# Long GpSimd operations in pieces of 256 elements, and two tiles of a top-k search decided on ScalarE

## The chip, the cores and the metric

The kernel runs on one core of a Trainium2 chip. The metric is the device time of one execution in microseconds. A core has a matrix engine (TensorE, PE in the profile), two elementwise engines (VectorE, DVE; GpSimd, POOL), an engine for activation functions (ScalarE, ACT) and a queue that issues most transfers (SP). Each engine works through its own instructions in order and waits on semaphores for the others.

## The reference, cut to what matters

A trunk of two layers over 1024 tokens of width 1024. Layer 0 projects the tokens and feeds two groups of heads: RWKV-7 (a recurrence over chunks of 64 tokens) and sparse attention, in which an index score selects at most 256 keys for each query. Layer 1 is gated linear attention. Each layer ends with an output projection and a layer norm.

The part that the change's second edit touches is the selection:

```python
score = jnp.einsum('bqh,bqhs->bqs', wib, jax.nn.relu(jnp.einsum('bqhd,bsd->bqhs', qib, ki)))
score = jnp.where(adm[None], score, -jnp.inf)      # only keys of the same or an earlier chunk of 64
vals, idx = lax.top_k(score, top_k)                # top_k = 256
...
s = jnp.where(valid[:, :, None, :], s, -1e30)
p = jax.nn.softmax(s, axis=-1)
```

The first edit touches elementwise work in all stages: the split of fp32 weights into a rounded part and a rest, decayed operands, masks, the shift at the end of a layer norm.

## The kernel before, in words

Weights and activations are split into two float32r parts, `hi` and `lo`, and a product takes three matmuls (L143 to L145, L165 to L167, L728 to L730). ScalarE rounds `hi` (L128) and GpSimd subtracts (L129), 128 x 512 at a time, in `wload`; in `wcols` (blocks of 8 x 128 columns) GpSimd does both, L153 and L154. Of both there are a few buffers, so a split is made ahead of the matmuls that read it.

Layer 0 runs in this order. Index scores and queries (until L441; the rests of the queries' split are L344 and L424 on GpSimd). Then the RWKV projections for four pairs of heads j: `proj` fills two PSUM banks (`dn`), ScalarE copies them out (L471, or L461 for a gate), DVE adds the shifted part (L472) or forms the gate (L462). `norms`, `decays` and `operands` make the chunks' decayed operands; L553 and L556 there are GpSimd's. Pairs 0 to 2 stand in the program before the top-k search, pair 3 and three gates behind it (L693 to L711).

The search (`search`, L631 to L654) finds, for each query of the tiles 2 to 7 of 128 queries, the largest threshold that at least 256 keys reach. It works on ordered integer keys, 16 bits at a time, so it is called twice (L656, L664), with 16 bits each. For each bit and each of the tiles 2 to 5, DVE counts the keys that reach the trial threshold (L641); two small operations then keep or drop the bit for all four tiles (L645, L646). For the tiles 6 and 7 ScalarE counts, by a sum of signs (L650), and DVE decides with two one-element operations per tile (L652, L653), for which ScalarE's next count of that tile waits. Behind the search DVE makes the selection's mask `bias_s` (L684 to L691).

Then come attention and the RWKV chunks, interleaved by hand (`att`, `slot`): `substitute` masks on GpSimd (L950, L972) around a chain of small GpSimd operations (L964, L965); head norms (`normed_heads`, L1075) run on DVE with `rsqrt` (L107 to L119), a chain of small operations. Output projection, layer norm (`normed`, L732: the last addition, L744, is GpSimd's), layer 1 with its gates (`gate_piece`, L1354 on GpSimd), output projection and layer norm end the kernel.

The order of the instructions on each engine is not the program's: `tile.TileContext(nc, schedule_with_timeline_sim=True)` (L1471) lets a planner lay them out by priority (the program's order) and by its own prices, so projections and the search are interleaved on DVE and ScalarE.

The lines of the search that the change edits:

```python
A.activation(ajunk[:, :n], x, AF.Sign, bias=c[:, z:z + 1], accum_out=cnt[:, z:z + 1])        # L650
V.tensor_scalar(step[:, zz], cnt[:, zz], float(2 * TOPK - n), bit, op0=ALU.is_lt, op1=ALU.mult)   # L652
V.scalar_tensor_tensor(c[:, zz], step[:, zz], -dn, c[:, zz], op0=ALU.add, op1=ALU.add)       # L653
```

Of the kernel before, what the change touches and what calls it, by code (L numbers as in the profile page):

```python
# [8 lines left out]
F32 = mybir.dt.float32  # L9
# [4 lines left out]
AF = mybir.ActivationFunctionType  # L14
ALU = mybir.AluOpType
AX = mybir.AxisListType
# 2 pi in parts: the products of the first two with an integer below 2^16 are exact
# [46 lines left out]
def trunk(ctx: ExitStack, tc: tile.TileContext, x, positions, e_w_in, a_mu, a_w0, a_w2, a_a0, a_a2,  # L64
# [7 lines left out]

    def dump(name, ap):
        if dbg and name in dbg:
            nc.sync.dma_start(dbg[name], ap)
# [31 lines left out]
    def rsqrt(pool, xin, n, tag):  # L107
        """1 / sqrt(xin) for positive xin, [P, n]"""
        y = pool.tile([P, n], F32, name=tag + "y", tag=tag + "y", bufs=2)
        xh = pool.tile([P, n], F32, name=tag + "h", tag=tag + "h", bufs=2)  # L110
        u = pool.tile([P, n], F32, name=tag + "u", tag=tag + "u", bufs=2)
        V.tensor_scalar(u.bitcast(I32), xin.bitcast(I32), 1, None, op0=ALU.logical_shift_right)
        V.tensor_scalar(y.bitcast(I32), u.bitcast(I32), -1.0, float(0x5f3759df), op0=ALU.mult, op1=ALU.add)
        V.tensor_scalar(xh, xin, -0.5, None, op0=ALU.mult)
        for _ in range(3):
            V.tensor_mul(u, y, y)
            V.tensor_mul(u, u, xh)
            V.scalar_tensor_tensor(y, u, 1.5, y, op0=ALU.add, op1=ALU.mult)  # L118
        return y  # L119

    # ================= weights: streamed, split exactly into two float32r parts =================
    def wload(wr, w, c0, n, k, raws=3, bufs=9, scale=None, sub=G):
# [4 lines left out]
        if scale is None:  # L127
            A.copy(hi, raw)  # L128
            sub.tensor_sub(lo, raw, f32(hi))  # L129
        else:  # L130
            A.activation(hi, raw, AF.Copy, scale=scale(k))
            V.scalar_tensor_tensor(lo, raw, scale(k), f32(hi), op0=ALU.mult, op1=ALU.subtract)
# [5 lines left out]
    def mm_fm(pst, wb, cs, ah, al, half):  # L138
        """pst [cols, 512] = w[:, cols]^T act[half]"""
# [7 lines left out]
    def wcols(pool, w, c0):  # L147
        """128 columns of w"""
# [5 lines left out]
        G.tensor_sub(lo, raw, f32(hi))  # L154
# [14 lines left out]
    def transpose_split(src, ah, al, t, k0=0, nk=NK, banks=("tr", "tr")):  # L169
        """src [128 tokens, nk*128] into the feature-major split pair at token tile t"""  # L170
# [10 lines left out]
    # scratch in DRAM  # L181
# [11 lines left out]
    # ================= layer 0 =================  # L193
# [103 lines left out]
    def rope(X, nt, nh, half, t0, step):  # L297
        """X [P, nt, nh, head dim], rotated in place"""
# [40 lines left out]
    def index_queries(t):  # L339
# [4 lines left out]
        EN[QSE[0]].tensor_sub(qs[:, :, 1], qb, f32(qs[:, :, 0]))  # L344
# [68 lines left out]
    def queries(t0, wb):  # L413
# [6 lines left out]
        for t in range(4):  # L420
# [3 lines left out]
            EN[QSE[1]].tensor_sub(qs[:, :, 1], q3, f32(qs[:, :, 0]))  # L424
# [67 lines left out]
    def spill(dst, us, j, src):  # L492
        """the odd heads' halves change places"""
        nc.sync.dma_start(dst[0:CH, j, us, :], src[0:CH])
        for a, b in ((0, CH), (CH, 0)):
            nc.sync.dma_start(dst[CH:, j, us, a:a + CH], src[CH:, :, b:b + CH])
# [3 lines left out]
    def norms(j, k):  # L500
        """1 / the norms of the heads' keys, times the keys"""
# [12 lines left out]
    def decays(j, h, pool):  # L514
        """the rates and their running decays"""
# [16 lines left out]
    def operands(j, h, r, k, rn, dec, pool):  # L532
# [17 lines left out]
        if RK1:  # L550
            O(j, 7).tensor_mul(kk, r_, k_)
        # the chunks' decay, for the state's increments
        O(j, 6).tensor_mul(bk, bk, PC[:, j, h * 8:h * 8 + 8, None].to_broadcast([P, 8, P]))  # L553
        spill(d_bd, slice(h * 8, h * 8 + 8), j, bk)
        if not RK1:
            O(j, 7).tensor_mul(kk, r_, k_)  # L556
# [59 lines left out]
    nH = th.tile([P, NI], F32, name="nH")  # L616

# [13 lines left out]
    def search(data, c):  # L631
        """largest c with at least TOPK of data >= c; ACT's columns hold 1/2 - c"""
        V.memset(c[:, 0:ND], 0.0)
        V.memset(c[:, ND:], 0.5)
        for b in range(15, -1, -1):
# [7 lines left out]
            # c is tried with the bit set; it is taken back where too few are left  # L643
# [3 lines left out]
            for i in AT:  # L647
                x, z = data[:, rng(i)], i - 2
                n = P * (i + 1)
                A.activation(ajunk[:, :n], x, AF.Sign, bias=c[:, z:z + 1], accum_out=cnt[:, z:z + 1])  # L650
                zz = slice(z, z + 1)
                V.tensor_scalar(step[:, zz], cnt[:, zz], float(2 * TOPK - n), bit, op0=ALU.is_lt, op1=ALU.mult)  # L652
                V.scalar_tensor_tensor(c[:, zz], step[:, zz], -dn, c[:, zz], op0=ALU.add, op1=ALU.add)  # L653
        V.tensor_scalar(c[:, ND:], c[:, ND:], -1.0, 0.5, op0=ALU.mult, op1=ALU.add)  # L654
# [22 lines left out]
    for i in range(2, NT):  # L677
# [5 lines left out]
        # BIG where above the threshold, and for as many of its equals as are still needed, from the left; less BIG  # L683
# [48 lines left out]
    def normed(pool, z, gb):  # L732
        """z normalised in place"""
# [10 lines left out]
        G.tensor_add(z, z, gb[1])  # L744

# [16 lines left out]
    def att_logits(i, w):  # L762
        """exp of the selected logits less their maximum, and its sums; a generator of TensorE's bursts, in us"""
# [24 lines left out]
    def att_out(i, w):  # L788
# [9 lines left out]
        # the sums' inverses, along the features  # L798
# [31 lines left out]
    def attention():  # L830
        """every tile's output beside the next one's logits"""
# [25 lines left out]
    # source token by target token: after it, not before it  # L857
# [6 lines left out]
    # lane = row set * 64 + unit * 8 + parity * 4 + block; a lane holds the rows 2 m + set of its block  # L864
# [9 lines left out]
    # a row's own block  # L874
# [30 lines left out]
    def load_unit(u):  # L905
        """AT: a, r; in the other parity's rows k's products with a"""
# [15 lines left out]
    def products(u, cc):  # L922
        """the chunk's own products"""
# [21 lines left out]
    def substitute(u):  # L945
        """-(I + M)^-1: the 16 x 16 blocks on the diagonal by substitution, half of a block's rows per partition"""
# [3 lines left out]
        G.tensor_mul(mm, U_[u]["MAB"].rearrange("p v (b t) -> p v b t", t=HB), own_)  # L950
# [21 lines left out]
        G.tensor_mul(TT.rearrange("p v (b t) -> p v b t", t=HB), td[:, :, None, :].to_broadcast([P, 8, 4, HB]), own_)  # L972
# [5 lines left out]
    def offdiag(u, z):  # L978
        """the blocks above the diagonal: of 16 x 16 in those of 32 x 32, then of 32 x 32"""
# [43 lines left out]
    def chain(u, slot):  # L1023
        U = U_[u]
        Y = rt([P, 8, CH], "Y", 2)
        for cc in range(2):
# [16 lines left out]
            # rows: the odd heads' outputs, then the even heads'  # L1043
# [45 lines left out]
    def finish(t):  # L1089
        """the bonus and the gate"""  # L1090
# [3 lines left out]
        # the pair's heads lie behind one another, two pairs share the partitions  # L1094
# [19 lines left out]
    # the output projection, one tile of tokens by one half of the columns at a time; z before its layer norm  # L1114
# [149 lines left out]
    # ================= layer 1 =================  # L1264
# [10 lines left out]
    # gates of the decay: rank 16  # L1275
# [72 lines left out]
    def gate_piece(t, c, wb):  # L1348
# [5 lines left out]
        G.tensor_mul(vg[c][:, t], vg[c][:, t], o)  # L1354
# [120 lines left out]
```

## Time and profile before

| | |
|---|---|
| median of 3 runs | 1380.54 us (1375.79 to 1385.37) |
| profiled execution, its span from first to last instruction | 1379.4 us |
| busy: TensorE matmuls | 1243.3 us, 90% |
| busy: DVE | 847.8 us, 61% |
| busy: ScalarE | 564.0 us, 41% |
| busy: GpSimd | 421.1 us, 31% |
| mean granted TensorE clock | 0.949 of full speed |

For the profiled execution the span is what is recorded; what lies around it is not, and the runs' median is 1.1 us above it. The shares are means over stages with different limits: the stage between 187 and 450 us holds the search. A DVE row of a few hundred nanoseconds may overlap the next by some tens of nanoseconds, so what an instruction costs its queue is read from the distance of the starts.

### The profile page before, as it was taken

The page shows a single profiled execution, that of the slowest core. Times are in us where ns is not written, and L with a number is a line of the kernel's source. Part 1 is how long each engine was busy: PE and PEld are TensorE (multiplying, and loading weights), DVE is VectorE, ACT ScalarE, POOL GpSimd, SP SyncE. Part 2 cuts the span into 40 slices and gives each one's busy share as a digit, 9 for nine tenths or more (in the row PEclk, how much of TensorE's full clock was granted, in tenths as well). Part 3 has the DMA queues.
Part 4 walks back from the last instruction along what each step waited for, and adds up shares of the span by engine and source line. Part 5 has one row for each costly group of instructions (what it writes and reads, how often), then busy time and mean ns, then how long its engine had stood idle before and what let it go on. Part 6 is the DMA issues. An engine that isn't in the chain of part 4 may idle for free. (4 is left out here: it accounts for less than half of the span.)

```text
span 1379.4 us, 21874 instructions
## 1 busy us (share of the span) xinstructions
PE 1243.3 (90%) x8141; PEld 963.6 (70%) x8141; DVE 847.8 (61%) x2029; ACT 564.0 (41%) x1089; POOL 421.1 (31%) x532
## 2 busy tenths in 40 slices
PE   7997797887788988999999879899999999998996
PEld 6976585565566666677766658777578878887885
DVE  5345879999999456768767646683330114453665
ACT  5345757637532425555554432132551123333100
POOL 3313431341424351444444351153112221131122
PEclk9998798998899989999999989999899999999998
DMA  6102311431424378334433376561102220013131
GB/s 206 31 1 76 107 39 31 124 104 50 127 54 122 108 199 216 90 73 120 125 94 78 88 222 214 197 200 60 35 0 61 62 62 0 1 62 103 62 118 62
DMA packets 164634, 130.50 MB, mean 95 GB/s; under 512 B 61424, under 2 KB 138272, under 8 KB 164528
## 3 DMA queue, kind: packets, MB, share of 16 engines
q1 hardware_dynamic: 161728, 122.72, 30.9%
q10 hardware_dynamic: 2800, 6.39, 1.5%
q8 instruction: 64, 1.05, 0.3%
q14 instruction: 42, 0.34, 0.1%
HBM read 86.08 MB, written 42.99 MB: 94 GB/s over the span
## 5 line engine op out<-in xcount | busy, mean ns | idle before, releaser
L129 POOL TENSOR_TENSOR wlo<-wraw,whi 128x512 fp32r<-128x512 f32 (+1 forms) x80 | 100.7, 1275 | 191.2 <-ACT whi L128 126.5
L143 PE MATMUL dn<-xh,chi 128*128 128x512 f32 x336 | 137.6, 410 | 16.6 <-DVE sh L472 8.7
L145 PE MATMUL dn<-xh,clo 128*128 128x512 f32 x336 | 137.3, 409 | 0.0
L144 PE MATMUL dn<-xl,chi 128*128 128x512 f32 x336 | 136.8, 407 | 0.0
L128 ACT CAST whi<-wraw 128x512 fp32r<-128x512 f32 (+1 forms) x80 | 48.6, 613 | 130.9 <-PE dn L144 65.6
L143 PEld LDWEIGHTS dn<-xh,chi 128*128 128x128 f32 x336 | 65.8, 196 | 36.3 <-issue 11.3
L744 POOL TENSOR_TENSOR z<-z,ln 128x1024 f32<-128x1024 f32 x16 | 38.7, 2419 | 166.6 <-DVE z L743 83.2
L144 PEld LDWEIGHTS dn<-xl,chi 128*128 128x128 f32 x336 | 65.9, 196 | 20.9 <-issue 7.4
L145 PEld LDWEIGHTS dn<-xh,clo 128*128 128x128 f32 x336 | 65.8, 196 | 18.6 <-issue 5.0
L153 POOL CAST chi<-craw 128x1024 fp32r<-128x1024 f32 x21 | 25.8, 1231 | 133.3 <-PE dn L144 95.3
L380 DVE SCALAR_TENSOR_TENSOR sc<-rl,wi_s,sc 128x384 f32<-128x384 f32 (+5 forms) x42 | 50.6, 1205 | 24.4 <-ACT rl L375 22.4
L728 PE MATMUL s<-whi,yh 128*128 128x512 f32 x128 | 52.6, 412 | 14.0 <-DVE gny L118 7.1
L795 PE MATMUL po<-pT,v_tm 128*64 128x256 f32 x288 | 62.7, 400 | 0.0
L785 ACT ACTIVATE p<-p,am 128x128 f32<-128x128 f32 (+7 forms) x64 | 49.1, 769 | 18.6 <-DVE am L783 18.1
L154 POOL TENSOR_TENSOR clo<-craw,chi 128x1024 fp32r<-128x1024 f32 x21 | 54.5, 2595 | 0.9
L776 DVE CUSTOM_DVE_ANT_0 p<-s,bias_s 128x512 f32<-128x512 f32 (+1 forms) x80 | 45.4, 591 | 14.8 <-PE s L775 11.9
L729 PE MATMUL s<-wlo,yh 128*128 128x512 f32 x128 | 52.2, 408 | 0.3 <-POOL wlo L129 0.3
L641 DVE TENSOR_SCALAR_CACHE_REDUCE junk<-klo,Lc 128x384 bf16<-128x384 int16 (+1 forms) x64 | 51.8, 809 | 0.6
L641 DVE TENSOR_SCALAR_CACHE_REDUCE junk<-khi,Hc 128x384 bf16<-128x384 int16 (+1 forms) x64 | 51.8, 809 | 0.5
L1354 POOL TENSOR_TENSOR vg<-vg,sg 128x512 f32<-128x512 f32 x16 | 20.5, 1285 | 103.2 <-DVE vg L1399 66.8
L165 PE MATMUL gt<-whi,hh 128*128 128x512 f32 x128 | 51.9, 406 | 0.0
L730 PE MATMUL s<-whi,yl 128*128 128x512 f32 x128 | 51.5, 402 | 0.0
(470 smaller groups left out, 3429.1 us busy)
## 6 DMA issues: line engine op xcount, KB each, us to landing
wraw<-in_o_w_in_dram SPq DMA_DIRECT2D x48, 256.0 KB
craw<-in_e_w_in_dram SPq DMA_DIRECT2D x21, 512.0 KB
xt<-in_x_dram SPq DMA_DIRECT2D x8, 512.0 KB
d_q<-qiT SPq DMA_DIRECT2D x8, 512.0 KB
d_ar<-ar SPq DMA_DIRECT2D x8, 512.0 KB
d_gate<-sg SPq DMA_DIRECT2D x8, 512.0 KB
qT<-d_q SPq DMA_DIRECT2D x8, 512.0 KB
BK<-d_bk SPq DMA_DIRECT2D x8, 512.0 KB
```

The lines of the kernel that those rows point to most:

```text
L129: sub.tensor_sub(lo, raw, f32(hi))
L143: PE.matmul(pst, wh[:, cs], ah[:, k, sl], start=(k == 0), stop=False)
L144: PE.matmul(pst, wh[:, cs], al[:, k, sl], start=False, stop=False)
L145: PE.matmul(pst, wl[:, cs], ah[:, k, sl], start=False, stop=(k == NK - 1))
L154: G.tensor_sub(lo, raw, f32(hi))
L165: PE.matmul(pst, ah[:, k, sl], wh, start=(k == 0), stop=False)
L380: E.scalar_tensor_tensor(acc[:, a:b], r, w, acc[:, a:b], op0=ALU.mult, op1=ALU.add)
L641: V.tensor_scalar(junk[:, :n], x, c[:, z:z + 1], None, op0=ALU.is_ge, op1=ALU.add, accum_out=cnt[:, z:z + 1])
L728: PE.matmul(pt, yh[:, k, :], wh, start=(k == 0), stop=False)
L729: PE.matmul(pt, yh[:, k, :], wl, start=False, stop=False)
L730: PE.matmul(pt, yl[:, k, :], wh, start=False, stop=(k == NK - 1))
L795: inorder(PE.matmul(po[RS[s], c:c + PVN], v_tm[:, kt, :], pT[s][:, c:c + PVN], start=(kt == 0 and c == 0), stop=(kt == i), skip_group_chec ...
```

## The change

First edit: GpSimd's two-input operations of 512 or 1024 elements a partition are issued in pieces of at most 256 elements: `cut` slices the first free dimension. It applies to L129 (2 pieces, 80 calls), L154 (4, 21), L344 and L424 (2, 6 and 8), L553 (4, 8), L556 (2, 8), L744 (4, 16), L950 and L972 (2, 8 each) and L1354 (2, 16). GpSimd's one-input operations (L153, L544) and the small ones stay.

Second edit: for the tiles 6 and 7 of the search, L652 and L653 on DVE become two activations on ScalarE, on one element a partition. A constant column `odd` holds n - 2 * 256 + 1, so that the sign of count plus `odd` is never zero; half a bit times that sign is taken from the threshold.

```diff
+    PIECE = 256
+    def cut(f, out, *ins):
+        n = out.shape[1]
+        each = 1
+        for m in out.shape[2:]:
+            each *= m
+        w = max(1, PIECE // each)
+        for a in range(0, n, w):
+            f(out[:, a:min(n, a + w)], *(z[:, a:min(n, a + w)] for z in ins))
+    def gsub(out, a, b):
+        cut(G.tensor_sub, out, a, b)
...
-            sub.tensor_sub(lo, raw, f32(hi))
+            gsub(lo, raw, f32(hi))
...
-        G.tensor_sub(lo, raw, f32(hi))
+        gsub(lo, raw, f32(hi))
...
-        EN[QSE[0]].tensor_sub(qs[:, :, 1], qb, f32(qs[:, :, 0]))
+        gsub(qs[:, :, 1], qb, f32(qs[:, :, 0]))
...
-        O(j, 6).tensor_mul(bk, bk, PC[:, j, h * 8:h * 8 + 8, None].to_broadcast([P, 8, P]))
+        (gmul if j < OG[6] else V.tensor_mul)(bk, bk, PC[:, j, h * 8:h * 8 + 8, None].to_broadcast([P, 8, P]))
...
+    sg_ = th.tile([P, NI], F32, name="sg_")
+    odd = th.tile([P, NI], F32, name="odd")
+    for i in AT:
+        V.memset(odd[:, i - 2:i - 1], float(P * (i + 1) - 2 * TOPK + 1))
...
-                A.activation(ajunk[:, :n], x, AF.Sign, bias=c[:, z:z + 1], accum_out=cnt[:, z:z + 1])
                 zz = slice(z, z + 1)
-                V.tensor_scalar(step[:, zz], cnt[:, zz], float(2 * TOPK - n), bit, op0=ALU.is_lt, op1=ALU.mult)
-                V.scalar_tensor_tensor(c[:, zz], step[:, zz], -dn, c[:, zz], op0=ALU.add, op1=ALU.add)
-        V.tensor_scalar(c[:, ND:], c[:, ND:], -1.0, 0.5, op0=ALU.mult, op1=ALU.add)
+                A.activation(ajunk[:, :n], x, AF.Sign, bias=c[:, zz], accum_out=cnt[:, zz])
+                A.activation(sg_[:, zz], cnt[:, zz], AF.Sign, bias=odd[:, zz])
+                A.activation(c[:, zz], sg_[:, zz], AF.Identity, scale=-0.5 * bit, bias=c[:, zz])
+        V.tensor_scalar(c[:, ND:], c[:, ND:], -1.0, None, op0=ALU.mult)
...
-        G.tensor_add(z, z, gb[1])
+        gadd(z, z, gb[1])
```

## Rows read from the trace of the kernel before

**Rows 1.** The page's 40 slices of the span, busy tenths of TensorE and of DVE.

```profile
PE   7997797887788988999999879899999999998996
DVE  5345879999999456768767646683330114453665
```

**Rows 2.** Busy time by stretch. After the stretch: its length, then busy us and instructions of TensorE, its weight loads, DVE, ScalarE and GpSimd; the granted clock, the DMA share and GB/s.

```profile
187.00:292.00 105.00, 91.59 (x359) 68.47 (x358) 103.55 (x270) 66.62 (x103) 29.75 (x18) 0.92 0.27 77
292.00:391.00 99.00, 78.59 (x276) 56.30 (x275) 97.26 (x261) 58.69 (x92) 30.80 (x18) 0.86 0.33 93
391.00:450.00 59.00, 51.04 (x198) 36.45 (x197) 57.29 (x86) 15.13 (x20) 21.98 (x11) 0.97 0.31 90
450.00:500.00 50.00, 49.48 (x198) 36.01 (x199) 23.59 (x29) 16.68 (x22) 20.05 (x12) 1.00 0.47 121
...
850.00:960.00 110.00, 101.05 (x458) 81.07 (x458) 75.98 (x160) 25.45 (x46) 36.43 (x22) 0.98 0.47 154
```

**Rows 3.** TensorE's longest waits between 187 and 450 us: who waited for whom, us in total, times, longest.

```profile
PE ix L508 <- ACT sq L506: 11.2, 2, 7.2
PE dn L143 <- DVE sh L472: 8.7, 2, 5.3
```

**Rows 4.** Timeline of DVE within one bit of the first search: start us, duration us, engine, line, operation, tiles and shapes.

```profile
207.17 0.15 DVE L652 TENSOR_SCALAR step<-cnt 128x1 f32<-128x1 f32 x1
207.29 0.75 DVE L641 TENSOR_SCALAR_CACHE_REDUCE junk<-khi,Hc 128x512 bf16<-128x512 int16 x1
...
207.96 0.15 DVE L653 SCALAR_TENSOR_TENSOR Hc<-step,Hc 128x1 f32<-128x1 f32 x1
208.08 0.88 DVE L641 TENSOR_SCALAR_CACHE_REDUCE junk<-khi,Hc 128x640 bf16<-128x640 int16 x1
...
210.06 0.17 DVE L645 TENSOR_SCALAR step<-cnt 128x4 f32<-128x4 f32 x1
210.26 0.16 DVE L646 SCALAR_TENSOR_TENSOR Hc<-step,Hc 128x4 f32<-128x4 f32 x1
```

**Rows 5.** DVE's groups between 187 and 391 us, those of the decisions: busy us, mean ns of one, then idle before.

```profile
L645 DVE TENSOR_SCALAR step<-cnt 128x4 f32<-128x4 f32 x31 | 12.0, 387 | 0.1
L653 DVE SCALAR_TENSOR_TENSOR Lc<-step,Lc 128x1 f32<-128x1 f32 x32 | 10.2, 320 | 0.0
...
L653 DVE SCALAR_TENSOR_TENSOR Hc<-step,Hc 128x1 f32<-128x1 f32 x32 | 6.9, 216 | 0.0
...
L646 DVE SCALAR_TENSOR_TENSOR Hc<-step,Hc 128x4 f32<-128x4 f32 x16 | 5.5, 346 | 0.2
...
L646 DVE SCALAR_TENSOR_TENSOR Lc<-step,Lc 128x4 f32<-128x4 f32 x15 | 4.8, 322 | 0.1
```

**Rows 6.** Timeline of ScalarE in two places, for small and dependent instructions: L529 reads what L528 writes; L785 has a bias column and a sum.

```profile
415.20 0.64 ACT L528 ACTIVATE ld<-ld 128x520 f32<-128x520 f32 x1
415.87 0.20 ACT L529 COPY PC<-ld 128x8 f32<-128x8 f32 x1
...
507.67 0.39 ACT L785 ACTIVATE p<-p,am 128x128 f32<-128x128 f32 x1
```

**Rows 7.** ScalarE's groups between 187 and 391 us, the counts of the tiles 6 and 7: busy us, mean ns, then idle before and whom it waited for.

```profile
L650 ACT ACTIVATE ajunk<-klo,Lc 128x896 bf16<-128x896 int16 (+1 forms) x32 | 35.0, 1093 | 26.8 <-DVE Lc L653 13.9 <-DVE step L652 6.2 <-DVE klo L663 5.1
L650 ACT ACTIVATE ajunk<-khi,Hc 128x896 bf16<-128x896 int16 (+1 forms) x32 | 35.0, 1092 | 17.7 <-DVE Hc L653 10.6 <-DVE step L652 5.1 <-DVE step L645 1.1
```

**Rows 8.** Timeline of all engines around 204 us, GpSimd's and DVE's rows.

```profile
203.98 2.39 POOL L154 TENSOR_TENSOR clo<-craw,chi 128x1024 fp32r<-128x1024 f32 x1
...
204.18 2.22 DVE L645 TENSOR_SCALAR step<-cnt 128x4 f32<-128x4 f32 x1
```

**Rows 9.** The counts of the first search on DVE: duration in ns, minimum, median and maximum, then first and last start and the forms.

```profile
L641 DVE TENSOR_SCALAR_CACHE_REDUCE junk<-khi,Hc x64: 599/798/1014, 187.7 to 284.8; 128x384 bf16<-128x384 int16 x16, 128x512 bf16<-128x512 int16 x16, 128x640 bf16<-128x640 int16 x16, 128x768 bf16<-128x768 int16 x16
```

**Rows 10.** Timeline around 813 us, GpSimd's and DVE's rows. The first row is five instructions in one block.

```profile
809.68 6.20 POOL L129 TENSOR_TENSOR wlo<-wraw,whi 128x512 fp32r<-128x512 f32 x5 [1.09 <-ACT whi L128]
...
812.72 0.75 DVE L1084 TENSOR_SCALAR var<-var 128x8 f32<-128x8 f32 x1
...
813.50 1.19 DVE L112 TENSOR_SCALAR gnu<-var 128x8 int32<-128x8 int32 x1
...
814.61 1.30 DVE L114 TENSOR_SCALAR gnh<-var 128x8 f32<-128x8 f32 x1
```

**Rows 11.** GpSimd's groups of the whole span, by form: busy us, mean ns of one, idle before and its releasers.

```profile
L129 POOL TENSOR_TENSOR wlo<-wraw,whi 128x512 fp32r<-128x512 f32 x72 | 92.0, 1295 | 175.8 <-ACT whi L128 111.1 <-PE dn L144 64.2
L154 POOL TENSOR_TENSOR clo<-craw,chi 128x1024 fp32r<-128x1024 f32 x21 | 54.5, 2595 | 0.9
...
L1042 POOL TENSOR_TENSOR SP<-RUV,PC 64x256 f32<-64x256 f32 x28 | 17.3, 617 | 33.1 <-DVE RUV L1066 28.1 <-DVE RUV L1064 4.0
```

**Rows 12.** Timeline of GpSimd at the end of the span.

```profile
1373.59 2.34 POOL L744 TENSOR_TENSOR z<-z,ln 128x1024 f32<-128x1024 f32 x1 [8.22 <-issue]
```

**Rows 13.** DVE's groups between 391 and 450 us, the two widest tiles of the selection's mask.

```profile
L691 DVE SCALAR_TENSOR_TENSOR bias_s<-gt__3235,sc 128x895 bf16<-128x895 f32 x1 | 3.2, 3216 | 0.0
L688 DVE SCALAR_TENSOR_TENSOR gt__3235<-gt__3235,sc 128x896 f32<-128x896 f32 x1 | 2.7, 2715 | 0.0
...
L691 DVE SCALAR_TENSOR_TENSOR bias_s<-gt__3243,sc 128x1023 bf16<-128x1023 f32 x1 | 1.6, 1641 | 0.0
...
L688 DVE SCALAR_TENSOR_TENSOR gt__3243<-gt__3243,sc 128x1024 f32<-128x1024 f32 x1 | 1.5, 1455 | 0.0
```

More of the change, by code (lines that the diff above doesn't have):

```diff
@@ L71, in trunk, with gmul, gadd @@
     CPY = [{"A": A.copy, "G": G.tensor_copy, "V": V.tensor_copy}[z] for z in CP]
+    PIECE = 256
[9 more added lines that the diff above has]
+        cut(G.tensor_sub, out, a, b)
+    def gmul(out, a, b):
+        cut(G.tensor_mul, out, a, b)
+    def gadd(out, a, b):
+        cut(G.tensor_add, out, a, b)
     def dump(name, ap):
@@ L119, in rsqrt, with wload @@
         return y
-    def wload(wr, w, c0, n, k, raws=3, bufs=9, scale=None, sub=G):
+    def wload(wr, w, c0, n, k, raws=3, bufs=9, scale=None):
         raw = wr.tile([P, 512], F32, name="wraw", tag="wraw", bufs=raws)[:, :n]
@@ L423, in queries @@
             CPY[1](qs[:, :, 0], q3)
-            EN[QSE[1]].tensor_sub(qs[:, :, 1], q3, f32(qs[:, :, 0]))
+            gsub(qs[:, :, 1], q3, f32(qs[:, :, 0]))
             qT = t1.tile([P, 8, P], F32R, name="qiT", tag="qiT", bufs=2)
@@ L550, in operands @@
         if RK1:
-            O(j, 7).tensor_mul(kk, r_, k_)
-        O(j, 6).tensor_mul(bk, bk, PC[:, j, h * 8:h * 8 + 8, None].to_broadcast([P, 8, P]))
+            (gmul if j < OG[7] else V.tensor_mul)(kk, r_, k_)
+        (gmul if j < OG[6] else V.tensor_mul)(bk, bk, PC[:, j, h * 8:h * 8 + 8, None].to_broadcast([P, 8, P]))
         spill(d_bd, slice(h * 8, h * 8 + 8), j, bk)
         if not RK1:
-            O(j, 7).tensor_mul(kk, r_, k_)
+            (gmul if j < OG[7] else V.tensor_mul)(kk, r_, k_)
         return kk
@@ L949, in substitute @@
         mm = rt([P, 8, 4, HB], "mm")
-        G.tensor_mul(mm, U_[u]["MAB"].rearrange("p v (b t) -> p v b t", t=HB), own_)
+        gmul(mm, U_[u]["MAB"].rearrange("p v (b t) -> p v b t", t=HB), own_)
         md = rt([P, 8, HB], "md")
@@ L971, in substitute @@
         TT = rt([P, 8, CH], "TT", 3)
-        G.tensor_mul(TT.rearrange("p v (b t) -> p v b t", t=HB), td[:, :, None, :].to_broadcast([P, 8, 4, HB]), own_)
+        gmul(TT.rearrange("p v (b t) -> p v b t", t=HB), td[:, :, None, :].to_broadcast([P, 8, 4, HB]), own_)
         U_[u]["TT"] = TT
@@ L1353, in gate_piece @@
         V.scalar_tensor_tensor(o, o, 1.0, pt, op0=ALU.add, op1=ALU.mult)
-        G.tensor_mul(vg[c][:, t], vg[c][:, t], o)
+        gmul(vg[c][:, t], vg[c][:, t], o)
     def vh(t, h):
```

## The prediction

> **What bounds the kernel now.** I read the slices of the page first, then busy time by stretch, then the waits of TensorE, then DVE instruction by instruction. TensorE is busy for 90% of the span, so the question is where its holes are and who makes them. In the slices (34.5 us each) DVE stands at 9 from about 207 to 448 us, where TensorE stands at 7 and 8 [rows 1]. By stretch [rows 2]: from 187 to 391 us, the whole of the two bit searches, DVE is busy 103.55 + 97.26 = 200.8 of 204 us; TensorE 170 and ScalarE 125.3. From 391 to 450 DVE is still busy 57.3 of 59. From 450 to 500 it is TensorE, 49.5 of 50. TensorE's waits between 187 and 450 us go to DVE and ScalarE, not to a DMA: 11.2 us for `sq` (ScalarE, itself behind DVE's `sh`) and 8.7 us for `sh` [rows 3]. So DVE's queue sets the pace from 187 to 450 us, and whatever leaves it there can shorten the kernel, until ScalarE or TensorE takes over.
>
> **Edit 1, ScalarE decides.** It takes L652 and L653 out of DVE's queue for two tiles, 16 bits and two searches: 64 of each. Undisturbed, each delays the next count by 0.12 us: L652 starts at 207.17 and the next count at 207.29, L653 at 207.96 and the count at 208.08 [rows 4]. 128 x 0.12 = 15.4 us. L653 is also held at times: its 32 calls in the first search take 6.9 us, in the second 10.2 us, against 0.15 us for a free one, so 17.1 - 64 x 0.15 = 7.5 us of holding [rows 4, 5]. What holds it is edit 2's matter; without L653 part of that falls on the next instruction, so I count 5 of the 7.5. DVE gains some 20 us.
>
> ScalarE gets 128 one-element instructions, each dependent on the one in front. No such form is in the trace. Below stands the copy of 8 elements, 0.20 us; above, an activation with a bias column over 128 elements, 0.39 us; a dependent one starts 0.03 us after its source ends (415.20 + 0.64, then 415.87) [rows 6]. Bounds 0.23 and 0.42, taken 0.32: the second without most of its elements. That makes 29 to 54 us, taken 41. Against it stands what goes away: ScalarE is idle 17.7 + 26.8 = 44.5 us in front of its counts, mostly for L653 and L652 [rows 7]. So ScalarE's queue is not clearly relieved: work of 125.3 us becomes 166, and the other idle time of that stretch, 204 - 125.3 - 44.5 = 34 us, is waits for DVE and TensorE. ScalarE alone would need between 166 (all of these go) and 200 us (none does). Behind a waiting small instruction stand the copies out of PSUM (L471, L461, L521) on which TensorE's banks depend.
>
> The Trainium skill speaks against this edit: "ScalarE: Activation LUTs", section "Rules for kernel authors", gives adds, multiplies and the like to VectorE, and the section "What ACT_TABLE_LOAD costs" prices an activation with a bias column at 280 ns plus 0.833 ns an element. By it (an estimate from that page) the 128 would cost 36 us, and the stretch would be bounded at 161 to 195 us by ScalarE; no row here shows a one-element activation.
>
> **Edit 2, pieces.** GpSimd's long instructions hold DVE up. L154 runs from 203.98 to 206.37; L645, which handles 4 elements in 0.17 us when free, starts at 204.18 and takes 2.22 us, to 206.40 [rows 4, 8]. Counts (L641) are never held: the longest of 64 takes 1.01 us, as one of the widest does [rows 9]. So the operations held are tensor_scalar on fp32 in SBUF and those with two SBUF inputs. Between 187 and 391 us L645 takes 12.0 us, where 31 free ones make 5.3, and L646 10.3, where 31 make 5.0: 12 us of holding beside L653's [rows 4, 5]. Does DVE get in between pieces that stand back to back? Rows 10 say so: five L129 run as one block from 809.68, 1.24 us apart, with borders at 813.40, 814.64 and 815.88; DVE's L1084, L112 and L114 end at 813.47, 814.69 and 815.91, one let in at every border. With pieces of 256, some 0.6 to 0.7 us each, a single held instruction waits about 0.35 us instead of about 1.2; but L645 and L646, one behind the other, are held by one piece each. So I take half of the 12 us: 6 us. Bounds: 0 (the second takes what the first saves) and 9.
>
> GpSimd's own price: 512 elements take 1.295 us, 1024 take 2.595 (with holding), and 256 elements on 64 partitions 0.617 [rows 11]. Twice 0.617 is 1.23, no more than one of 512; a line through the free lengths of L129 in its block, 1.24, and of the last L744, 2.34 [rows 10, 12], leaves 0.14 us that every further piece would add. 134 instructions become two and 45 become four, so 269 further pieces cost 0 to 38 us on an engine busy 31%. Nearly all lies behind buffers. Open to view are the last addition of the kernel (2.34 us, 3 more pieces: 0 to 0.4 us, [rows 12]) and the two masks of each unit's substitution; taken together 1 us of loss.
>
> **The sum.** From 187 to 391 DVE would need 204 - 20 - 6 = 178 us, ScalarE 166 to 200. Two queues in order that wait on each other end above the fuller one's work; I take 184, nearer to DVE's end, since ScalarE's other waits are mostly for DVE: 20 us saved. Ends: 204 - 178 + 4 = 30, if the rest of the holding goes too, and 4. From 391 to 450 the masks after the search are held as well: the 895-element L691 took 3.22 us where the longer one of 1023 took 1.64, L688 2.72 against 1.46 [rows 13], 2.8 us at least; two thirds of that goes, 2 us (0 to 6, since shorter ones are held too). From 450 to 500 TensorE is full: nothing to gain, and the time saved before passes through whole only if its work there doesn't grow. TensorE itself has room: 170 busy of 204 [rows 2]. Behind 800 us the head norms' chain is held by 0.58 + 1.02 + 1.13 us (their lengths in [rows 10] less 0.17 each); half goes, 1.4 us; in the layer norm stretch TensorE is busy 101 of 110 [rows 2] and I count nothing. Less the 1 us of loss: 20 + 2 + 1.4 - 1 = 22.4. The profiled span is 1379.4 us, the median of the runs 1380.5, 1.1 above it. 1379.4 - 22.4 + 1.1 = 1358 us.
>
> **Rivals.**
> A. Everything that leaves DVE becomes time: 30 in the search, 6 behind it, 5 in the norms: 1380.5 - 41 = 1339. For it: DVE at 98%. Against: ScalarE's 166 us and more.
> B. The gain is given back before the attention starts. The order of instructions on each engine is laid out by a planner with its own prices (L1471), and from 450 on TensorE is full. If the planner puts the same projections at the same distance behind the search, only some 5 us arrive: 1375. For it: the 49.5 of 50 us. Against: the waits of rows 3 are DVE's.
> C. The pieces don't do what they say: GpSimd keeps hold over a row of pieces. Then the 6, the 2 and the 1.4 go: 1380.5 - 14 + 1 = 1367. Against: rows 10.
> D. ScalarE becomes the bound. At 0.42 us a small instruction and none of the other 34 us gone the stretch is 125.3 + 54 + 34 = 213 us, 9 longer than now, and with 1 us of GpSimd and some 2 us of later PSUM copies 1380.5 + 12 = 1392. It decides from 0.35 us for each small instruction on: (204 - 125.3 - 34) / 128. For it: the chain count, sign, identity is serial on one queue. Against: waits on DVE, 44.5 us, leave the same queue. This is where the rule of the Trainium skill named above ("ScalarE: Activation LUTs", "Rules for kernel authors") would lead.
>
> **How the numbers follow.** Forecast 0.55 (own range 1346 to 1367), A 0.12, B 0.16, C 0.09, D 0.08. A measurement here tells about 1%, 13.8 us, from no change: faster is below 1366.7. Forecast nearly whole (0.53), A and half of C: 0.69. Slower is a small half of D and little else: 0.05. Same: 0.26. Range 1336 to 1380: it leaves out D and a little below A, and takes in both ends of the sums.
>
> **What would show it.** The second search ends before 375 us instead of 391, and DVE stays over 95% busy to its end. L645 and L646 together fall from 22 to about 16 us. No DVE instruction of a few elements takes over 1 us beside a run of pieces. ScalarE's busy time in the search stretch rises by 30 to 50 us, with no wait on DVE in front of its counts; one small activation takes 0.25 to 0.35 us. Attention's first logits start some 20 us earlier than now, and the distance from there to the end is unchanged within 3 us. It is wrong if ScalarE is over 95% busy in the search and DVE idles for the two tiles at the end of a search (D), if held instructions are as long as now (C), or if the search ends early and TensorE's work up to the attention doesn't (B).

## The result and the profile after

The changed kernel takes 1344.4 us (median of 4 runs, 1342.4 to 1349.5) against 1380.8 for the kernel before in the same rounds (4 runs): ratio 0.9735, 95% interval 0.9698 to 0.9773, 36 us less. The forecast was 1358 in 1336 to 1380. The profiled span is 1344.1 us, 35.3 less than before.

In the changed kernel line numbers are 21 to 27 higher: the counts on DVE are L667 (before L641), the decisions L671 and L672 (L645, L646), ScalarE's count, sign and identity L677, L678 and L679, the index scores' additions L401 (L380), GpSimd's whole casts L174 (L153), and all pieces L83.

The page's slices, to lay beside [rows 1]:

```profile
PE   7998898888899989989999699999999999998996
DVE  5346789999997557677766526881601124453665
```

DVE's run of nines is one slice shorter, from 202 to 403 us instead of 207 to 448. How far each stretch moved is seen by the first and last instruction of its own line in the two traces:

```
stretch (us in the profiled execution)              before   after   moved
start to the first count of the search               187.7    176.3   -11.3
first count to the last one                          204.8    191.4   -13.4
last count to attention's first logits               113.2    105.3    -7.8
first logits to the end of the span                  873.8    871.0    -2.8
span                                                1379.4   1344.1   -35.3
```

Busy time by stretch in the changed kernel, columns as in [rows 2]; the last two rows are the two searches:

```profile
72.40:165.00 92.60, 81.25 (x374) 62.43 (x373) 58.48 (x78) 59.63 (x102) 43.09 (x37) 0.93 0.20 69
176.40:267.90 91.50, 80.93 (x321) 61.09 (x320) 89.00 (x196) 70.99 (x158) 33.04 (x39) 0.94 0.26 75
267.90:367.80 99.90, 85.55 (x337) 63.73 (x336) 95.01 (x210) 74.65 (x167) 43.14 (x54) 0.95 0.38 102
```

and the first of these stretches in the kernel before, for which no row stands above:

```profile
72.40:165.00 92.60, 74.69 (x330) 57.61 (x329) 55.69 (x67) 55.30 (x95) 31.10 (x18) 0.86 0.20 68
```

In the searches DVE is busy 89.0 + 95.0 = 184.0 of 191.4 us, 96%, and still sets the pace. In the index stage, which the forecast left out, TensorE does 374 products where it did 330 in the same time. The window is fixed and the changed kernel is some us ahead in it; taken from the first of the index scores' additions to the last, the stage has 333 products in 94.8 us before and 359 in 89.3 after. TensorE's granted clock in the window, a mean between the levels of 1.2 and 2.4 GHz, rises from 0.86 to 0.93, and in the two searches it stands at 0.94 and 0.95 where stretches of before had 0.92 and 0.86 [rows 2]. It went up with the pieces in either order of the work (last section); by what, no run here shows.

What held instructions look like now. DVE's groups of the decisions in the searches, to lay beside [rows 5]:

```profile
L671 DVE TENSOR_SCALAR step<-cnt 128x4 f32<-128x4 f32 x32 | 10.3, 323 | 0.8
L672 DVE SCALAR_TENSOR_TENSOR Lc<-step,Lc 128x4 f32<-128x4 f32 x15 | 4.2, 278 | 0.3
L672 DVE SCALAR_TENSOR_TENSOR Hc<-step,Hc 128x4 f32<-128x4 f32 x16 | 3.8, 238 | 0.4
```

22.3 us have become 18.3. The longest L671 takes 1.01 us, and its cause is not a piece: it lies beside one of the whole one-input casts, which the change does not cut. GpSimd's and DVE's rows there:

```profile
259.25 1.04 POOL L174 CAST chi<-craw 128x1024 fp32r<-128x1024 f32 x1 [0.16 <-PE dn L165]
259.30 1.01 DVE L671 TENSOR_SCALAR step<-cnt 128x4 f32<-128x4 f32 x1
```

Beside pieces the picture is the one of [rows 10], at half the distance. First the kernel before, in the norm ahead of the index scores, then the changed one at the same place:

```profile
65.24 2.55 POOL L129 TENSOR_TENSOR wlo<-wraw,whi 128x512 fp32r<-128x512 f32 x2
65.35 1.20 DVE L116 TENSOR_TENSOR rsq8u<-rsq8y 128x8 f32<-128x8 f32 x1
66.59 1.22 DVE L117 TENSOR_TENSOR rsq8u<-rsq8u,rsq8h 128x8 f32<-128x8 f32 x1
```

```profile
63.80 3.33 POOL L83 TENSOR_TENSOR wlo<-wraw,whi 128x256 fp32r<-128x256 f32 x4
64.39 0.69 DVE L139 SCALAR_TENSOR_TENSOR rsq8y<-rsq8u,rsq8y 128x8 f32<-128x8 f32 x1
65.11 0.65 DVE L137 TENSOR_TENSOR rsq8u<-rsq8y 128x8 f32<-128x8 f32 x1
65.80 0.66 DVE L138 TENSOR_TENSOR rsq8u<-rsq8u,rsq8h 128x8 f32<-128x8 f32 x1
```

DVE is let in once at every border, and the border now comes after 0.7 us instead of 1.25. The Trainium skill, "SBUF — State Buffer", section "Who interferes with whom", has this as an exclusive lock: a DVE instruction with two SBUF inputs, or in a two-port mode, contends with GpSimd, and whichever came first keeps the shared ports for its whole instruction. The held rows here agree with the lock and its length; which mode L671 runs in, no row shows.

ScalarE's groups in the searches, to lay beside [rows 7]: busy us, mean ns, then idle before.

```profile
L678 ACT ACTIVATE sg__2847<-cnt,odd 128x1 f32<-128x1 f32 x64 | 18.1, 283 | 0.1
L677 ACT ACTIVATE ajunk<-klo,Lc 128x896 bf16<-128x896 int16 x16 | 16.5, 1032 | 4.6 <-DVE klo L689 4.6
L677 ACT ACTIVATE ajunk<-khi,Hc 128x896 bf16<-128x896 int16 x16 | 16.5, 1032 | 0.0
L679 ACT ACTIVATE Hc<-sg__2847,Hc 128x1 f32<-128x1 f32 x32 | 9.1, 284 | 0.0
```

No count stands idle for a decision any more. Of TensorE's longest waits between 176 and 418 us, to lay beside [rows 3], that for `sq` has gone from 11.2 us to 2.3.

```profile
PE ix L541 <- DVE kk L585: 6.8, 2, 4.1
PE dn L164 <- DVE sh L493: 6.3, 2, 5.9
...
PE ix L529 <- ACT sq L527: 2.3, 1, 2.3
```

### The profile page after: what moved, and what is told of

Read it like the earlier page. It is cut to its first block, busy times and chain, and to the rows that moved or that the text cites. A ratio compares the mean times of both kernels' runs of the same rounds, so it can differ in the third digit from the quotient of the medians.

```text
span 1344.1 us, 22146 instructions
## 1 busy us (share of the span) xinstructions
PE 1232.1 (92%) x8141; PEld 953.5 (71%) x8141; DVE 814.5 (61%) x1903; ACT 583.0 (43%) x1217; POOL 492.6 (37%) x801
## 5 line engine op out<-in xcount | busy, mean ns | idle before, releaser
L83 POOL TENSOR_TENSOR wlo<-wraw,whi 128x256 fp32r<-128x256 f32 (+1 forms) x160 | 116.4, 757 | 160.0 <-ACT whi L149 118.0
L83 POOL TENSOR_TENSOR z<-z,ln 128x256 f32<-128x256 f32 x64 | 47.2, 769 | 158.3 <-DVE z L769 51.0
L83 POOL TENSOR_TENSOR clo<-craw,chi 128x256 fp32r<-128x256 f32 x84 | 77.9, 957 | 1.0
L83 POOL TENSOR_TENSOR vg<-vg,sg 128x256 f32<-128x256 f32 x32 | 24.2, 776 | 99.5 <-DVE vg L1425 54.5
L401 DVE SCALAR_TENSOR_TENSOR sc<-rl,wi_s,sc 128x384 f32<-128x384 f32 (+5 forms) x42 | 45.2, 1076 | 24.2 <-ACT rl L396 21.8
L174 POOL CAST chi<-craw 128x1024 fp32r<-128x1024 f32 x21 | 23.1, 1099 | 94.6 <-PE dn L165 77.9
L837 PE MATMUL st<-ident,p 128*128 128x128 f32 x288 | 50.1, 290 | 4.5 <-ACT pT L839 3.1
L667 DVE TENSOR_SCALAR_CACHE_REDUCE junk<-khi,Hc 128x384 bf16<-128x384 int16 (+1 forms) x64 | 51.8, 810 | 1.7
L667 DVE TENSOR_SCALAR_CACHE_REDUCE junk<-klo,Lc 128x384 bf16<-128x384 int16 (+1 forms) x64 | 51.8, 810 | 1.7
```

The costliest lines, as they stand in the source:

```text
L83: f(out[:, a:min(n, a + w)], *(z[:, a:min(n, a + w)] for z in ins))
L667: V.tensor_scalar(junk[:, :n], x, c[:, z:z + 1], None, op0=ALU.is_ge, op1=ALU.add, accum_out=cnt[:, z:z + 1])
L837: inorder(PE.transpose(pt[:, j * P:(j + 1) * P], ps[2 * j + s][:, kt * P:(kt + 1) * P], ident))
```

## The experiments

Line numbers in the edits are those of the kernel before. "Old order" and "new order" mean that each engine's instructions are held to a given sequence by order-only edges between neighbours, without a wait. This matters because the kernel's own planner lays out all engines afresh when GpSimd's calls change. Kernels not so held are laid out afresh. In the expectations, first and second edit are those of the section on the change. Every ratio is to runs of the kernel before in the same rounds, medians 1380.5 to 1381.8 us. The stretches of all fourteen traces, worked out as in the table above:

```
us                      to first  index scores  search  to first  rest
                        count     alone                 logits
before                  187.7     94.8          204.8   113.2     873.8
pieces_only             176.6     89.5          196.2   113.8     873.0
scalar_only             187.6     95.2          199.8   105.5     867.2
pieces_old_plan         181.9     91.2          193.7   114.2     873.7
l154_old_plan           186.2     92.3          196.9   114.0     867.5
whole_new_plan          185.3     91.4          208.3   115.5     873.6
both_512                187.7     94.1          191.1   105.1     872.4
both_128                183.0     95.6          187.3   111.6     864.2
both_one_input          177.8     90.7          186.8   108.0     879.6
one_input_pinned        177.4     91.1          188.5   107.3     870.1
scalar_plus_dummies     179.1     89.3          199.7   105.8     871.7
queries_whole           179.3     88.9          191.4   108.3     873.6
odd_width               178.5     89.3          192.5   106.9     874.7
after                   176.3     89.3          191.4   105.3     871.0
```

Each row is one execution, so a difference of a few us is uncertain; the last column goes from 864 to 880 though most of the edits change little there. Up to the first count TensorE goes through its products in one of two orders, as the traces show: the old one in before, scalar_only, pieces_old_plan, l154_old_plan and both_512, the new one in whole_new_plan, pieces_only, scalar_plus_dummies, queries_whole, one_input_pinned, odd_width and the whole change. both_one_input differs a little from the new one, and both_128 has a third.

**pieces_only: GpSimd's pieces alone.** (The edit is the diff above without its search part.)

> The first edit alone (all pieces, DVE decides for the two tiles as before), planned afresh. Theory H (holding): pieces shorten what GpSimd holds on DVE; of the 36 us of the whole change this part has the index scores' 9, part of the search and the later stages: 1380 - 22 = 1358 us (1350 to 1366). Rival P (plan): the planner moves about half of TensorE's instructions when the pieces are there, and that is what gains: 1358 here as well; the two pinned kernels tell them apart. Rival C (GpSimd keeps hold over a row of pieces): 1375 or more.

Measured: 1358.95 us (1356.9 to 1361.6), ratio 0.9839 (0.9809 to 0.9868): 22 us of the 36.

**scalar_only: ScalarE's decisions alone.** (The search part of the diff alone.)

> The second edit alone (ScalarE decides, long GpSimd operations whole). H: the search stretch loses 128 x 0.12 = 15 us of DVE's queue and a part of L653's holding, and nothing changes before and after it: 1380 - 15 = 1365 us (1360 to 1370). If ScalarE is the bound: 1378 or more.

Measured: 1368.04 us (1361.8 to 1371.1), ratio 0.9896 (0.9863 to 0.9928): 13 us. 22 + 13 = 35, so the two add up and neither needs the other. The time is in the range expected, but half of the reasoning fails: by its trace 5.0 us of the gain lie in the search and 7.7 between the last count and the logits, where nothing was to change. The profiled execution was the fastest of this kernel, so the 6.6 us that it shows behind the first logits are not to be read as a gain.

**pieces_old_plan: the pieces, in the old order.**

```diff
-            sub.tensor_sub(lo, raw, f32(hi))
+            cut(sub.tensor_sub, lo, raw, f32(hi))
...
+        tc.add_manual_dep(i, last.name, NoSync)   # each engine, sequence of the kernel before
```

> The first edit alone, with every engine's instructions pinned to the order that the planner gave the kernel before (a piece stands where its whole operation stood). H: the gain of the pieces is in the holding, so it stays: within 5 us of the pieces planned afresh, about 1360. P: the gain was the plan's: 1376 to 1384.

Measured: 1363.39 us (1361.8 to 1366.9), ratio 0.9870 (0.9839 to 0.9902): 18 of the 22 us come without any instruction changing its place.

**whole_new_plan: no pieces, in the order that the planner makes with pieces.**

```diff
+        tc.add_manual_dep(i, last.name, NoSync)   # each engine, sequence of pieces_only
```

> The kernel before (whole GpSimd operations, DVE decides), with every engine's instructions pinned to the order that the planner gives the kernel with pieces (a whole operation stands where its last piece stood). H: 1376 to 1386, no gain without pieces. P: about 1358, the gain without any piece.

Measured: 1379.44 us (12 runs, 1376.4 to 1387.1), ratio 0.9992 (0.9968 to 1.0016): nothing. The new order alone is worth no time; with pieces it adds some 4 us. So the pieces themselves are the cause. That they work by holding DVE for less is seen in the rows: with the order held, DVE's decisions L645, L646 and L653 take 30.8 us in the searches instead of 39.9. Another way would be that TensorE starts sooner on a split whose first part is ready; but in the kernel before, TensorE waits between 70 and 510 us for GpSimd only 4.0 us in all, for `kk` of L556, and with pieces in the old order this wait is longer, 8.9 us.

**l154_old_plan: only L154 in pieces, in the old order.**

```diff
-        G.tensor_sub(lo, raw, f32(hi))
+        cut(G.tensor_sub, lo, raw, f32(hi))       # L154; all other calls whole
```

> Pieces of 256 in L154 alone (the projections' weight rest, 21 operations of 1024 elements), DVE decides, order pinned to that of the kernel before. H: L154 is what holds DVE in the search (its 12 there are 29.7 us of GpSimd's 61), so two thirds of the 18 us of all pieces in that order: 1369 us (1364 to 1374). If the gain came from the index scores and the later stages: 1376 or more.

Measured: 1367.2 us (1364.7 to 1370.1), ratio 0.9899 (0.9871 to 0.9926): 13 of the 18 us from 21 instructions of 532, those of 1024 elements, 12 of which run beside the search. By its one trace the search is 7.9 us shorter; the 6.3 us that the trace shows behind the first logits, where no L154 runs, can't be told from chance.

**both_512 and both_128: the whole change with another length.**

```diff
-    PIECE = 256
+    PIECE = 512      # both_512: only calls of 1024 are cut
+    PIECE = 128      # both_128
```

> The whole change with pieces of 512: only the operations of 1024 elements (L154, L553, L744) are cut, in two. H: half of what the pieces of 256 brought, between the second edit alone (1368) and the whole change (1344): 1356 us (1350 to 1362). If any cut at all does it (a border to get in at is what counts): 1346.

> The whole change with pieces of 128 elements instead of 256. H (holding sets the gain, in proportion to a piece's length): held DVE instructions wait half as long again, GpSimd gets 448 more pieces at up to 0.14 us, 0 to 63 us on an engine busy 37% after the change: 1340 us (1335 to 1347). If GpSimd's own price per piece decides: 1350 or more.

Measured: 512 takes 1357.45 us, ratio 0.9828 (0.9802 to 0.9853); 128 takes 1343.81, ratio 0.9726 (0.9698 to 0.9754), the same as 256. The table shows where 512 loses its 13 us: its search is as short as with 256, but it starts as late as before, at 187.7 us. The length is not all that differs there: 512 goes up to the first count in the old order of TensorE's work, 256 in the new. In the old order pieces of 256 bring the first count forward by 5.8 us (pieces_old_plan) and those of 512 by nothing; the other 5.6 us of the 11.4 come with the new order, or are chance. In the index stage its granted clock and products are nearly the old ones:

```profile
72.40:165.00 92.60, 74.67 (x335) 57.24 (x333) 56.00 (x66) 54.97 (x93) 32.36 (x21) 0.89 0.19 64
```

That 128 is no faster than 256 is a balance in its traces: the search is 4.1 us shorter and starts 6.7 later, with an index stage of 95.6 us in which TensorE, in another order, does 374 products, against 359 in 89.3 us.

The decisions' longest instances go with the piece: L645 is held up to 2.31 us before, up to 1.27 with 512, 1.01 with 256 (beside a cast) and 0.65 with 128. The kernel before, then 512, then 128; the numbers behind the count are minimum, median and maximum in ns:

```profile
L645 DVE TENSOR_SCALAR step<-cnt x32: 148/169/2308, 198.2 to 392.5; 128x4 f32<-128x4 f32 x32
```

```profile
L645 DVE TENSOR_SCALAR step<-cnt x32: 144/170/1270, 197.2 to 378.9; 128x4 f32<-128x4 f32 x32
```

```profile
L645 DVE TENSOR_SCALAR step<-cnt x32: 157/170/646, 191.7 to 370.4; 128x4 f32<-128x4 f32 x32
```

**queries_whole: L344 and L424 left whole, everything else as in the whole change and in its order.**

```diff
-        cut(EN[QSE[0]].tensor_sub, qs[:, :, 1], qb, f32(qs[:, :, 0]))
+        EN[QSE[0]].tensor_sub(qs[:, :, 1], qb, f32(qs[:, :, 0]))
```

> The whole change, with every engine's order as in it, but L344 and L424 (the low parts of the index queries and of the attention's queries, 14 calls of 512 elements in all, the only cut two-input operations besides L129 and L154 before 190 us) left whole. It is to tell whether the gain ahead of the search comes from these. Theory 1: with pieces of 512, where these two were also whole, the index scores ended at 171.1 us instead of 161.7, and with only L154 in pieces at 168.8, so it is these two: the scores end 4 to 8 us later than in the whole change (166 to 170), L380 takes 49 to 50 us instead of 45.2, and the time is 1349 to 1353. Theory 2: it is the fresh order of the instructions, which this run keeps: the scores end within 1.5 us of 161.7, the time is 1343 to 1346.

Measured: 1349.17 us (1339.3 to 1354.4), ratio 0.9750 (0.9714 to 0.9786). By its median alone Theory 1 would stand, though its interval overlaps that of the whole change (0.9698 to 0.9773); its mechanism falls: L380 takes 48.5 us, as theory 1 has it, and yet the stretch of the index scores is no longer than in the whole change, 88.9 against 89.3. The 3 us by which everything is later are there before the first score (75.7 us against 72.4), and the first score lies anywhere from 72.0 to 77.1 us over all these traces. So the two calls are not shown to be the cause. By single traces, pieces in the old order shorten that stretch by 3.6 us, the new order alone by 3.4, and both together by 5.3.

**both_one_input and one_input_pinned: the one-input operations in pieces too, planned afresh and in the whole change's order.**

```diff
-        CPY[0](hi, raw)
+        cut(CPY[0], hi, raw)                      # L153, and L544 likewise
```

> The whole change, and GpSimd's one-input operations in pieces of 256 as well: the rounding cast of wcols (L153, 1024 elements) and L544 (512). H, if one-input operations hold DVE as two-input ones do: 1341 (1336 to 1346). If they hold nothing: 1344 to 1348, the price of 71 more pieces.

> One-input operations (L153, L544) in pieces of 256 too, on top of the whole change, with every engine pinned to the order that the planner gave the whole change. If the 6 us that these pieces cost when planned afresh (1350 against 1344) were the plan's: 1340 to 1346. If they are the price of 71 more pieces in front of TensorE's weights: 1348 to 1352.

Measured: 1350.0 us, ratio 0.9776 (0.9748 to 0.9804), and 1346.79, ratio 0.9765 (0.9738 to 0.9792). No gain in time: the first lies above both ranges expected, the second between its two, and with the order held the interval overlaps that of the whole change. Casts do hold DVE a little: in one order the search takes 188.5 us with them cut and 191.4 in both traces with them whole (after, queries_whole). That 2.9 us doesn't arrive at the end; the start, 1.1 us later, and the stretch behind the search, 2.0 longer, take it up.

**scalar_plus_dummies: the whole change, and on DVE two instructions in the place of L652 and L653 whose results nobody reads.**

```diff
+                V.tensor_scalar(dum[:, 2:3], c[:, 0:1], 1.0, bit, op0=ALU.is_lt, op1=ALU.mult)
+                V.scalar_tensor_tensor(dum[:, 3:4], c[:, 1:2], -dn, dum[:, 0:1], op0=ALU.add, op1=ALU.add)
```

> The whole change, with two one-element operations put back into DVE's queue for each tile and bit, of the forms of L652 and L653, on columns of their own that nothing reads; ScalarE still decides. Theory S (DVE's slots are what the second edit gains): 128 x 0.12 = 15 us come back, 1359 us (1355 to 1364). Rival W (the gain is that ScalarE no longer waits for DVE's answer): 1344 to 1349.

Measured: 1357.62 us (1353.7 to 1361.6), ratio 0.9840 (0.9815 to 0.9864): 13 us given back. That is Theory S's range and not rival W's. DVE's groups between 179 and 379 us:

```profile
L653 DVE SCALAR_TENSOR_TENSOR dum<-Hc,dum 128x1 f32<-128x1 f32 x32 | 9.5, 298 | 0.0
...
L653 DVE SCALAR_TENSOR_TENSOR dum<-Lc,dum 128x1 f32<-128x1 f32 x30 | 6.8, 228 | 0.0
...
L653 DVE TENSOR_SCALAR dum<-Hc 128x1 f32<-128x1 f32 x32 | 4.8, 148 | 0.5
L653 DVE TENSOR_SCALAR dum<-Lc 128x1 f32<-128x1 f32 x30 | 4.4, 148 | 0.4
```

The one with two inputs takes 16.3 us for 62, where 62 free ones make 9.3: 7.0 us of holding, and the search is 8.3 longer than in the changed kernel. The one with one input is never held. Of the other 5 us, 2.8 lie ahead of the search, where there is no dummy and TensorE's order is that of the whole change; the traces with that order and pieces of 256 put the first count anywhere from 176.3 to 179.3 us, so this may be chance. The total fits the 15 us of slots that the forecast counted, and for another reason. Between two counts a free instruction takes no time at all. The kernel before, where no L653 stands between the counts of 512 and 640 elements:

```profile
201.41 0.75 DVE L641 TENSOR_SCALAR_CACHE_REDUCE junk<-khi,Hc 128x512 bf16<-128x512 int16 x1
202.08 0.08 DVE L641 DVE_READ_ACCUMULATOR junk<-khi,Hc 128x1 f32 x1
202.20 0.88 DVE L641 TENSOR_SCALAR_CACHE_REDUCE junk<-khi,Hc 128x640 bf16<-128x640 int16 x1
```

and the changed one:

```profile
193.46 0.75 DVE L667 TENSOR_SCALAR_CACHE_REDUCE junk<-khi,Hc 128x512 bf16<-128x512 int16 x1
194.13 0.08 DVE L667 DVE_READ_ACCUMULATOR junk<-khi,Hc 128x1 f32 x1
194.25 0.88 DVE L667 TENSOR_SCALAR_CACHE_REDUCE junk<-khi,Hc 128x640 bf16<-128x640 int16 x1
```

From count to count it is 0.79 us in both, and 0.79 in [rows 4] with L653 between them (207.29 to 208.08). Over the kernel before, the median gap from the end of one count to the start of the next is 0.04 us with nothing between (21 places), with L652 (26) and with L653 (17). The 0.12 us belong to the count's own accumulator read, beside which the small instruction runs. Behind L645 or L646 it is the same: to the next count 0.20 us with a small instruction between (11 places) and without (12). Only beside a longer instruction or another small one does it add 0.06 to 0.07 us, at some 40 of the 128 places, 3 us in all at most.

**odd_width: L645 on five columns instead of four.**

```diff
-            V.tensor_scalar(step[:, lo], cnt[:, lo], float(TOPK), -bit, op0=ALU.is_lt, op1=ALU.mult)
+            V.tensor_scalar(step[:, 0:ND + 1], cnt[:, 0:ND + 1], float(TOPK), -bit, op0=ALU.is_lt, op1=ALU.mult)
```

> The whole change, with L645 on five columns instead of four (one unused column between DVE's and ScalarE's). L652, on one column, was never held before the change (0.128 to 0.152 us), L645, on four, was (up to 2.3). If an even number of columns is what gets it held: no L645 over 0.25 us, DVE 5 us freer, 1340 us (1337 to 1343). If more than one column is: L645 up to 0.9 us as now, 1344 (1341 to 1347).

Measured: 1350.66 us (1345.4 to 1355.6), ratio 0.9783 (0.9753 to 0.9812). The time is above both ranges; the kernel is laid out afresh. An odd width does not keep the instruction from being held:

```profile
L645 DVE TENSOR_SCALAR step<-cnt x32: 144/172/892, 187.6 to 371.1; 128x5 f32<-128x5 f32 x32
```

## Why the prediction came out as it did

The prediction numbers the edits the other way round from the section on the change: its edit 1 is ScalarE's deciding, its edit 2 the pieces. This section follows it.

Side and stated range held, but the gain was 36 us where 22.4 were forecast: 1344.4 lies below the forecast's own 1346 to 1367 and nearer to rival A's 1339 than to 1358. A's reason does not hold for it: A had 30 us saved in the search, and the search gave 13.4. The mechanism was the right one, GpSimd's length and DVE's queue, but two steps were wrong and partly made up for each other, and one stretch was missing; that the time came out in the range is partly luck.

**"128 x 0.12 = 15.4 us" was nearly nothing.** The step took the time from L652's start to the next count's start for L652's price. The same 0.12 us stand between two counts that have nothing between them, as the rows at 201.41 show; one look at such a pair in the trace of before would have told. What edit 1 took off DVE was mainly the holding of L653, put at 7.5 us, and the dummies' 7.0 bear that out.

**Edit 1 still brought 13 us**, in two parts. In its own trace the search is 5.0 us shorter. That part is DVE's: DVE is busy 8.1 us less in it (201.5 to 193.4), and putting back instructions for DVE alone, the dummies, made the search 8.3 us longer.

The other 7.7 us lie between the last count and the logits, and there the dummies take nothing back. That stretch is 105 to 112 us in the table's nine kernels that have edit 1, the dummies' among them, and 113 to 116 in the five without. So this part comes with ScalarE's deciding itself, the term that the forecast set at nothing clear, and not with DVE's time. How it comes about stays open. In the kernel before, TensorE's wait for `sq`, which stands behind ScalarE's counts, which wait for DVE's decisions, is 11.2 us; with edit 1 alone it is 5.7:

```profile
PE ix L508 <- ACT sq L506: 5.7, 1, 5.7
```

TensorE then does 653 products in the search instead of 637, so fewer are left for the stretch behind it. But there its matmuls are busy only 2.1 us less (99.9 to 97.8), and the rest of the 7.7 is shorter waiting; and both_one_input leaves as many products as the kernel before and still has 108.0 us. The planner's order, which edit 1 alters a little, is the other candidate; no run here separates them.

**ScalarE's price was too high.** One small activation takes 0.283 us (0.32 taken). The Trainium skill, "ScalarE: Activation LUTs", section "What ACT_TABLE_LOAD costs", has 280 ns plus 0.833 ns an element for it; the trace agrees. But they overlap with their neighbours, and ScalarE's busy time in the search rises by 21 us (124.6 to 145.6), not by 41. So D was far off. The Trainium skill, same page, section "Rules for kernel authors", gives such arithmetic to VectorE; here that is 13 us slower (scalar_only), with VectorE busy for 98% of the search before.

**Edit 2 was sized too small in the search.** Taken 6 + 2 us from 187 to 450; the pieces in the old order take 11.1 us off the search alone. 6.3 of that are L645 and L646, as forecast, and 2.8 are L653's holding, which the forecast gave to edit 1; larger two-input operations are held as well, of which only the masks were counted. In the whole change L645 and L646 fall to 18.3 us, where 16 were forecast. Rival C is out: the new order without pieces is worth nothing, the pieces in the old order 18 us.

**The stretch ahead of 187 us was left out**, and this is the largest miss: 11.3 of the 35.3 us. "From 187 to 450 DVE's queue sets the pace" was true but not all of it. From 76 to 171 us TensorE was busy for 81% too, at a granted clock of 0.86, and DVE's additions, with two SBUF inputs, were held there; nothing was costed. By the runs, pieces in the old order bring the search forward by 5.8 us and the new order alone by 2.4, both together by 11.1. The rest, 3 us, is not settled: the first score alone varies by 5 us from trace to trace.

**Search to logits and the rest.** The search and the masks together were forecast at 22 us, and search to logits came to 13.4 + 7.8 = 21.2: nearly the sum, by other parts than those counted. Behind the first logits 2.8 us were gained, no more than chance by the table; 1.4 less 1 was forecast. GpSimd's pieces cost what was said where they are free: the kernel's last addition takes 2.76 us instead of 2.34, 0.14 for each further piece. In all GpSimd is busy 492.6 us instead of 421.1, 0.27 for each of 269 further pieces; beside DVE four pieces take 3.33 us (at 63.80 above), in the last addition 2.76. No loss from it is seen at the end. B, the planner giving the gain back, did not happen: first logits start 32.5 us earlier and the distance behind them is 2.8 less.

## What to carry to other kernels

Where GpSimd works beside a DVE that sets the pace, cut GpSimd's long operations: the total work grows, but a held DVE instruction waits for the running piece only; go down in length until the longest held instance stops mattering. Here, with ScalarE deciding, 512 elements cost 13 us against 256, of which some 6 come with another order of the work, or by chance, and not with the length, and 128 brought no more than 256. Price a small instruction by comparing the same two neighbours with and without it, not by the distance from its start to the next one. And look for the mechanism in every stretch where its two engines run side by side, not only in the one where the engine is fullest.

## What the runs showed of the hardware that was not expected

- A one-column DVE instruction between two counts with a sum costs no time when it isn't held: gap 0.04 us with it and without it.
- A one-column tensor_scalar on fp32 in SBUF was never held (L652 at most 0.15 us, the dummies' mean 0.148), one on four or five columns is (up to 2.31 and 0.89 us); a one-column operation with two SBUF inputs is held as well.
- One-element activations that don't depend on each other start 0.19 us apart though each takes 0.28: an identity at 224.38 and a sign at 224.57 in the changed kernel.
- TensorE's mean granted clock from the first of the index scores' additions to the last went up with the pieces in either order: 0.86 to 0.91 in the old one (before, pieces_old_plan) and 0.87 to 0.92 in the new one (whole_new_plan, pieces_only).
- Edits that do little themselves, laid out afresh by the planner, came out up to 6 us above the whole change (1350.0 and 1350.7 against 1344.4; the first 1346.8 with the order held), which the intervals only just fail to separate; whoever compares versions of a planned kernel has to hold the order or allow for that.
